# A two-layer mixer and a two-layer transformer block in float32 on one core: x and ctx fetched ahead of the weights, conditioning in two 32-column parts, value products in runs of two pairs

## Chip, cores and metric

One core of a Trainium2 chip. The metric is the device time of one execution in microseconds: the median of three runs before is 1947.4 (1946.05 to 1948.95). Outputs are float32.

## What is computed

x and ctx have 256 tokens of 1024 features. A first block has two layers of this form (a second block follows with two rounds of ffn1, mix, ffn2; the last norm ends the kernel):

```
mod   = silu(c) @ ada_w + ada_b          # shift, scale, gate for x
mod_c = silu(c_ctx) @ ada_w + ada_b      # the same for ctx
hx = rmsnorm(x, norm_w) * (1 + scale) + shift        # hc likewise from ctx
px, pc = split(hx @ w_in), split(hc @ w_in)
ya = global attention; yb = neighbourhood attention; yc = window attention
x = x + gate * ((concat(ya, yb, yc) * silu(px[9])) @ w_out)   # ctx too, in layer 0
```

In the second block, mix has two attentions: N (a compressed branch over 16 blocks, a selected and a window branch, gated) and M (causal), each with 8 heads, merged through w_branch and w_out. The compressed keys and values come from a small network with the weights cmpk_w1, cmpv_w1 and w2.

## The kernel before

Weights are stored as one packed array in the order of `weight_plan` (lines 108 to 141), in tiles of 128 x 1024 floats (512 KB). `_dma` (248) issues one tile on SP's queue, `_split` (272) makes a rounded part wh with ScalarE (286) and a remainder wl with VectorE (287), up to AHEAD = 2 tiles ahead of their use with three buffers each. `three` (424 to 428) multiplies float32 numbers as three products of rounded parts, accumulated in PSUM; every large product is made of these lines 426, 427 and 428. Python code emits the program, and a scheduler may put an instruction earlier than the text has it, once its tiles are free; each engine then runs its own instructions in order.

**The start** (`start`, 833). SP's queue fetches two weight tiles, x, four tiles, ctx, two tiles, the constants, then tiles up to 18. x and ctx are normalized in place (842 to 844). The shift and scale of layer 0 come in two groups of two column blocks (`ADA_HALF`, 56), eight tiles each. The first group (tiles 0 to 7, `START_PLAIN`) multiplies unsplit float32 weights by a stationary operand of 8 columns (747), into 8 rows of one PSUM bank. The second group is split and uses two products (750, 752), interleaved with the gate projection of chunks 0 to 3 (`gate`, 851; 96 matmuls of line 424's kind in four banks over both halves). `ada_close` (756) copies the bank to SBUF (762), selects and transposes it with the constant sel2 (765) and adds the bias. `half` (846) transposes x and ctx (800), applies scale and shift (809) and splits the result into hT (812, 813), half of the feature chunks at a time. The later groups (`ADA_FILL`, 57) run inside layer 0's gate projections; two of them hold the gate part of the modulation.

**Attention** (`attention`, 502). A unit holds one or two slots of scores; two units make a pair of heads. For each slot: scores (514, 515), softmax (`f_m`, `f_n`), transposes of the weights into PSUM (580), a copy to the tile pt (596, 598; three buffers). `f_v` (600) multiplies pt by V for one pair: line 609, plain float32, two 64-column parts of the array in turn, into 256 columns of the single bank "o". It is called when both units of the pair have been copied, or in a loop behind the last slot (639, 644). In N, the second pair member adds the compressed branch (`extra`, 1372), products with 64 rows and 128 columns. Layer 0 has 4 bundles of 8 units and 4 of 4; layer 1 4 of 4 and 4 of 2; each mix 2 of 4 and 4 of 2. Attention, preparation and projections are interleaved by lanes with estimated costs (`q`, 306; `step`, 317).

**The end of a layer** (1097 to 1143). The gate of each stream is spread over 128 partitions by TensorE: 24 matmuls with a broadcast stationary column (1116) and VectorE copies (1117). Since the buffers of x and ctx serve as storage for the gate projection in layer 0 (`sg`, 888 to 892), both are fetched again (1110). `add` (1119) then multiplies and adds.

**The mix** (1188). The compression weights w1 (two loads of 1 MB in runs of 512 bytes, 1205) and w2 (1218) are issued on ScalarE's queue when the mix opens. `compress` (1227) uses them. fw2, the last norm's weight, is issued at the stage i = 1 (1516).

Of the kernel before, what the change touches and what calls it, by code (L numbers as in the profile page):

```python
# [15 lines left out]
ALU = mybir.AluOpType  # L16
# [43 lines left out]

START_TILES = 18
START_PLAIN = range(8)
START_LOADS = (2, 6, 8, START_TILES)
# [44 lines left out]
def weight_plan():  # L108
# [3 lines left out]
    n = len(a[1]) // 2  # L112
    plan += a[0] + g[0][:1] + a[1][:n] + g[0][1:] + a[1][n:] + g[1]
# [44 lines left out]
def const_table():  # L158
# [39 lines left out]
    e = np.arange(32)[:, None]  # L198
# [30 lines left out]
class Body:  # L229
# [272 lines left out]
    def attention(self, units, evac):  # L502
# [97 lines left out]
        def f_v(x):  # L600
            pair = units[x:x + 2]
            O = self.ps("o")[:, :2 * P]
            extra = pair[1].get("extra")
            nk = len(pair[0]["v"])
            for k in range(nk):
                for i in (1, 0):
                    u = pair[i]
                    v, b, m, c = u["v"][k]
                    nc.tensor.matmul(O[HD * i:HD * i + HD, c:c + m * P], v, u["pt"][:, b:b + m, :].rearrange("p m t -> p (m t)"),  # L609
                                     start=k == 0, stop=k == nk - 1 and extra is None)  # L610
            if extra is not None:
                extra(O)
            evac(O, pair[1])
# [13 lines left out]
        for s in range(n):  # L627
# [11 lines left out]
            while nv < len(units) and ends[nv + 1] < s:  # L639
                f_v(nv)  # L640
                c += 430 * len(units[nv]["v"])
                nv += 2
            yield c
        while nv < len(units):
            f_v(nv)
            nv += 2
            yield 430.0
# [91 lines left out]
    def ada_tile(self, g):  # L739
# [5 lines left out]
        for i, kk in enumerate(ks):  # L745
            if plain:
                self.nc.tensor.matmul(g["bank"][:4 * nb, :], self.cst1[:, kk, w], h[:, i, :],  # L747
                                      start=g["n"] == 0 and i == 0, stop=g["n"] == g["last"] and i == len(ks) - 1)
                continue
# [6 lines left out]
    def ada_close(self, g):  # L756
# [5 lines left out]
        nc.scalar.copy(m[:4 * nb, :], g["bank"][:4 * nb, :])  # L762
        p = self.ps("r")
        for j in range(4):
            nc.tensor.matmul(p[:, 16 * j:16 * j + 2 * nb], m[:4 * nb, j * P:(j + 1) * P],
                             self.cst("sel2")[:4 * nb, :2 * nb], start=True, stop=True)
        pv = p[:, :64].rearrange("p (j b s) -> p s b j", b=8, s=2)
        b = 0
        while b < nb:
# [4 lines left out]
            for s in range(2):  # L774
# [5 lines left out]
                if a < z:  # L780
                    nc.vector.scalar_tensor_tensor(self.mod[l][:, s, a:z], self.mod[l][:, s, a:z], 1.0,
                                                   self.col("norm_w", 8 * l + a - 8, z - a), op0=ALU.add, op1=ALU.mult)
            b = e

# [35 lines left out]
    def block1(self, x):  # L820
        nc, tc = self.nc, self.tc
        cx = self.cx1
        with ExitStack() as es:
            hp = es.enter_context(tc.tile_pool(reuse_waits="tile", name="hT", bufs=1))
            hT = self.new_hT(hp, 0)
            with tc.tile_pool(reuse_waits="tile", name="w0", bufs=START_TILES) as self.w0:
                self.start(x, cx, hT)
# [5 lines left out]
    def start(self, x, cx, hT):  # L833

        nc, tc = self.nc, self.tc
        for n, (t, nm) in zip(START_LOADS, ((x, "x"), (cx, "ctx"), (self.consts[0], "consts"), (None, None))):
            while self.di < n:
                self._dma()
            if nm:
                d = self.dram[nm]  # L840
                nc.sync.dma_start(t, d if nm == "consts" else d.rearrange("o (t p) d -> p (o t) d", p=P))
        nc.vector.tensor_copy(self.ident_r, self.ident)
        self.norm_rows(x, x)
        self.norm_rows(cx, cx)

        def half(h):
            for c in (4 * h, 4 * h + 2):
                for s, v in enumerate((x, cx)):
                    self.mod_pair(0, s, c, self.turn_pair(v, c), hT)

        def gate(h, i, n):
            ks, _, wh, wl = self.w_next("w_in", 0, 3072 + 256 * i)
            for a, kk in enumerate(ks):
# [3 lines left out]
                for _ in range(n):  # L857
                    yield

        self.fill, self.fills = None, list(ADA_FILL)  # L860
        g = self.ada_open(ADA_HALF[0], "m")
        for i in range(8):
            self.ada_tile(g)
        self.ada_close(g)
        half(0)
        self.gate_acc = [self.acc() for _ in range(GATE_HALF)]
        g = self.ada_open(ADA_HALF[1], "m")
        for i in range(GATE_HALF // 2):
            for _ in gate(0, i, 1):
                self.ada_tile(g)  # L870
        self.ada_close(g)
        self.cond1.close()
        half(1)
        for i in range(GATE_HALF // 2):
            for _ in gate(1, i, 0):
                pass
# [4 lines left out]
    def layer1(self, l, x, cx, hT, hp):  # L881
# [3 lines left out]
        with ExitStack() as lay:  # L885
            lp = lay.enter_context(tc.tile_pool(reuse_waits="tile", name=f"lay{l}", bufs=1))
            if need:
                sg2 = lp.tile([P, 4, T], F32, name="sg2")
                xv, cv = (t.rearrange("p t (a d) -> p (t a) d", d=T) for t in (x, self.cx1))

                def sg(c, n):
                    return (xv, cv, sg2)[c // 4][:, c % 4:c % 4 + n, :]
# [17 lines left out]
            sink = lp.tile([P, 8], F32, name=f"sink{l}")  # L910
# [3 lines left out]
            nsink = lp.tile([P, 8], F32, name=f"nsink{l}")  # L914
# [185 lines left out]
            with tc.tile_pool(reuse_waits="tile", name=f"wo{l}", bufs=1) as wp:  # L1100
                gate = wp.tile([P, 2, D], F32, name=f"gt{l}")
                tmp = wp.tile([P, 4, 512], F32, name=f"tmp{l}")
                if need:
# [5 lines left out]
                    for t, nm in ((x, "x"), (cx, "ctx")):  # L1109
                        nc.sync.dma_start(t, self.dram[nm].rearrange("o (t p) d -> p (o t) d", p=P))  # L1110
# [519 lines left out]
```

## Time and profile before

| | |
|---|---|
| profiled execution | 1947.63 us, span 1945.8 |
| TensorE | 1904.4 us busy, 98% |
| weight loads of TensorE | 1561.0 us, 80% |
| VectorE, ScalarE | 1279.4 us (66%), 1103.3 us (57%) |
| GpSimd | 1.0 us |
| granted clock, mean | 0.992 |
| DMA | 294.62 MB, 151 GB/s |

Times in the trace are microseconds from the first instruction. A matmul's end is modelled, and consecutive ones overlap, so the time that one takes of the engine is read from start to start.

### The profile page before, as it was taken

The page shows a single profiled execution, that of the slowest core. Times are in us where ns is not written, and L with a number is a line of the kernel's source. Part 1 is how long each engine was busy: PE and PEld are TensorE (multiplying, and loading weights), DVE is VectorE, ACT ScalarE, POOL GpSimd, SP SyncE. Part 2 cuts the span into 40 slices and gives each one's busy share as a digit, 9 for nine tenths or more (in the row PEclk, how much of TensorE's full clock was granted, in tenths as well). Part 3 has the DMA queues.
Part 4 walks back from the last instruction along what each step waited for, and adds up shares of the span by engine and source line. Part 5 has one row for each costly group of instructions (what it writes and reads, how often), then busy time and mean ns, then how long its engine had stood idle before and what let it go on. Part 6 is the DMA issues. An engine that isn't in the chain of part 4 may idle for free.

```text
span 1945.8 us, 27694 instructions
## 1 busy us (share of the span) xinstructions
PE 1904.4 (98%) x10348; PEld 1561.0 (80%) x10348; DVE 1279.4 (66%) x2490; ACT 1103.3 (57%) x1979; POOL 1.0 (0%) x7
## 2 busy tenths in 40 slices
PE   8999999999999999999899999999999899999998
PEld 3777778777988877888788878888888788888886
DVE  5486856788596787555689575555555588675555
ACT  4367657775567675444467645445444458655443
POOL 0000000000000000000000000000000000000000
PEclk9999999999999999999999999999999999999999
DMA  7333324135422236554523565554555433456552
GB/s 304 106 123 130 118 90 150 55 131 186 136 93 95 85 109 216 184 184 141 166 93 125 164 215 198 183 191 173 193 186 173 144 106 101 152 180 234 186 181 74
DMA packets 85270, 294.62 MB, mean 151 GB/s; under 512 B 10000, under 2 KB 10384, under 8 KB 85136
## 3 DMA queue, kind: packets, MB, share of 16 engines
q1 hardware_dynamic: 80432, 283.39, 43.0%
q10 hardware_dynamic: 4704, 9.47, 1.5%
q8 instruction: 81, 1.33, 0.3%
q14 instruction: 53, 0.43, 0.1%
HBM read 291.77 MB, written 1.05 MB: 150 GB/s over the span
## 4 chain that ended last, share of the span: by engine, by line
PE 92%; DVE 4%; ACT 2%; issue 1%; ACTq 1%; DMA 1%; SPq 0%; DVEq 0%
PE acc L426 24%; PE acc L428 24%; PE acc L427 24%; PE pso L609 4%; PE pst L580 4%; PE pss L514 2%; PE pss L515 2%; PE psr L715 1%; DVE wl L287 1%; PE psx L1173 1%; ACT wh L286 1%; PE psr L721 1%; PE psm L747 1%; PE psm L1260 1%; PE acc L750 1%
## 5 line engine op out<-in xcount | busy, mean ns | idle before, releaser
L287 DVE TENSOR_TENSOR wl<-ws,wh 128x1024 fp32r<-128x1024 f32 (+2 forms) x538 | 638.1, 1188 | 478.8 <-ACT wh L286 476.0
L286 ACT CAST wh<-ws 128x1024 fp32r<-128x1024 f32 (+2 forms) x538 | 549.2, 1024 | 573.3 <-PE acc L428 503.3
L426 PE MATMUL acc<-wh,xt 128*128 128x512 f32 (+3 forms) x1120 | 419.6, 376 | 11.7 <-ACT wh L286 11.7
L427 PE MATMUL acc<-wl,xt 128*128 128x512 f32 (+3 forms) x1120 | 416.6, 372 | 0.0
L428 PE MATMUL acc<-wh,xt 128*128 128x512 f32 (+3 forms) x1120 | 416.4, 373 | 0.0
L426 PEld LDWEIGHTS acc<-wh,xt 128*128 128x128 f32 x1120 | 212.1, 190 | 44.9 <-ACT wh L286 12.9
L428 PEld LDWEIGHTS acc<-wh,xt 128*128 128x128 f32 x1120 | 211.8, 189 | 33.0 <-issue 0.7
L427 PEld LDWEIGHTS acc<-wl,xt 128*128 128x128 f32 x1120 | 212.7, 190 | 31.2 <-issue 0.3
L426 PE MATMUL acc<-wh,hT 128*128 128x384 f32 (+2 forms) x480 | 159.6, 333 | 0.1
L427 PE MATMUL acc<-wl,hT 128*128 128x384 f32 (+2 forms) x480 | 158.5, 330 | 0.0
L428 PE MATMUL acc<-wh,hT 128*128 128x384 f32 (+2 forms) x480 | 158.1, 329 | 0.0
L550 ACT ACTIVATE p<-pss,nm 128x512 f32<-128x512 f32 (+2 forms) x240 | 127.5, 539 | 20.3 <-DVE nm L546 5.1
L426 PE MATMUL acc<-wh,hffn 128*128 128x512 f32 x352 | 137.7, 391 | 0.0
L428 PE MATMUL acc<-wh,hffn 128*128 128x512 f32 x352 | 137.1, 389 | 0.0
L427 PE MATMUL acc<-wl,hffn 128*128 128x512 f32 x352 | 137.0, 389 | 0.0
L580 PE MATMUL pst<-consts,p 128*128 128x128 f32 x624 | 103.3, 278 | 0.0
L427 PEld LDWEIGHTS acc<-wl,hT 128*128 128x128 f32 x480 | 90.6, 189 | 7.2 <-issue 1.9
L426 PEld LDWEIGHTS acc<-wh,hT 128*128 128x128 f32 x480 | 90.5, 189 | 6.8 <-issue 0.8
L428 PEld LDWEIGHTS acc<-wh,hT 128*128 128x128 f32 x480 | 90.5, 189 | 5.8 <-issue 1.2
L580 PEld LDWEIGHTS pst<-consts,p 128*128 128x128 f32 x624 | 72.2, 140 | 28.5 <-ACT p L572 5.6
L572 ACT ACTIVATE p<-p,rinv 128x256 f32<-128x256 f32 (+2 forms) x152 | 81.5, 573 | 16.5 <-DVE rinv L566 12.2
L428 PEld LDWEIGHTS acc<-wh,hffn 128*128 128x128 f32 x352 | 66.1, 188 | 13.9
(318 smaller groups left out, 2868.5 us busy)
## 6 DMA issues: line engine op xcount, KB each, us to landing
ws<-in_wall SPq DMA_DIRECT2D x476, 512.0 KB, 3.4
ws<-in_wall SPq DMA_DIRECT2D x64, 384.0 KB, 3.1
bias<-in_bias ACTq DMA_DIRECT2D x8, 512.0 KB, 4.0
x<-in_x SPq DMA_DIRECT2D x2, 1024.0 KB, 6.5
cx<-in_ctx SPq DMA_DIRECT2D x2, 1024.0 KB, 10.3
ws<-in_wall SPq DMA_DIRECT2D x4, 420.0 KB, 3.0
out<-y SPq DMA_DIRECT2D x2, 512.0 KB, 2.6
ws<-in_wall SPq DMA_DIRECT2D x2, 280.0 KB, 2.8
```

What stands on the lines that cost most here:

```text
L286: self.nc.scalar.copy(h[:, :n], s[:, :n])
L287: self.nc.vector.tensor_tensor(lo[:, :n], s[:, :n], h[:, :n].bitcast(F32), op=ALU.subtract)
L426: mm(out, ah, bh, start=start, stop=False)
L427: mm(out, ah, bl, start=False, stop=False)
L428: mm(out, al, bh, start=False, stop=stop)
L514: nc.tensor.matmul(S[:, o:o + w], q, kh, start=True, stop=False)
L515: nc.tensor.matmul(S[:, o:o + w], q, kl, start=False, stop=True)
L550: nc.scalar.activation(p[:, o:o + w], S[:, o:o + w], AF.Exp, bias=nm[:, i:i + 1], accum_out=sm[:, i:i + 1])
L572: nc.scalar.activation(p[:, o:o + w], p[:, o:o + w], AF.Copy, scale=r[:, i:i + 1])
L580: nc.tensor.transpose(t[:, i * P:(i + 1) * P], sl["P"][:, o:o + P], self.ident)
L609: nc.tensor.matmul(O[HD * i:HD * i + HD, c:c + m * P], v, u["pt"][:, b:b + m, :].rearrange("p m t -> p (m t)"), start=k == 0, stop=k == nk ...
L715: nc.tensor.transpose(p[:, 2 * a + g, :], ks[:, t, a, g, :], self.ident_r)
```

## The change

- Start: x, the identity part of the constants and ctx are fetched ahead of all weight tiles; the rest of the constants follows tile 8. Normalized rows go to new tiles, so x stays as it was. Both groups of layer 0 are plain float32; the two matmuls of a tile go to the column parts 0 to 31 and 32 to 63, into 64 rows, and sel2 (now 64 rows) adds the parts up. The order of tiles is first group, first gate tile, second group, the other gate tiles.
- Attention: `f_v` takes two pairs (four units) into the two halves of the bank, the second pair first; it is called once four units are ready. pt has five buffers. The compressed branch becomes products of 128 rows (zeros in 64 of them) and 64 columns inside the same run; its tiles are padded to 128.
- The gate rows are written to DRAM from POOL's queue (`gate_rows`) and read back as a broadcast on ScalarE's queue, in place of lines 1112 to 1117. x is not fetched again; ctx is.
- w1 and w2 are issued in ffn1, after its second wg product (`cmp_load`), into tiles of the second block's pool; fw2 at i = 2.

```
-START_PLAIN = range(8)
+START_PLAIN = [*range(8), *range(9, 17)]
...
-    plan += a[0] + g[0][:1] + a[1][:n] + g[0][1:] + a[1][n:] + g[1]
+    plan += a[0] + g[0][:1] + a[1] + g[0][1:] + g[1]
...
-                u["pt"] = self.pp.tile([P, 8, P], F32, tag="pt", name=f"pt_{self.uid}", bufs=3)
+                u["pt"] = self.pp.tile([P, 8, P], F32, tag="pt", name=f"pt_{self.uid}", bufs=5)
...
+        def f_v(x, n):
+            pairs = [(units[x + 2 * j], units[x + 2 * j + 1], 2 * P * j) for j in range(n)]
+            O = self.ps("o")
+            todo = []
+            for pair in pairs[::-1]:
+                for k in range(len(pair[0]["v"])):
+                    for i in (1, 0):
+                        v, b, m, c = pair[i]["v"][k]
+                        todo.append((i, c + pair[2], m * P, v, pair[i]["pt"][:, b:b + m, :].rearrange("p m t -> p (m t)")))
+            for pair in pairs[::-1]:
+                todo += [(i, c + pair[2], P, v, p) for i, c, v, p in pair[1].get("extra", [])]
+            for y, (i, c, w, v, p) in enumerate(todo):
+                nc.tensor.matmul(O[HD * i:HD * i + HD, c:c + w], v, p, start=y < 2, stop=y >= len(todo) - 2)
+            for pair in pairs:
+                evac(O[:, pair[2]:pair[2] + 2 * P], pair[1])
...
-            while nv < len(units) and ends[nv + 1] < s:
-                f_v(nv)
-                c += 430 * len(units[nv]["v"])
-                nv += 2
+            if nv + 3 < len(units) and ends[nv + 3] < s:
+                f_v(nv, 2)
+                c += 860 * len(units[nv]["v"])
+                nv += 4
...
+                g["rows"] = 64
+                self.nc.tensor.matmul(g["bank"][32 * i:32 * i + 32, :], self.cst1[:, kk, 28 - 4 * b:60 - 4 * b], h[:, i, :],
+                                      start=g["n"] == 0, stop=g["n"] == g["last"])
...
+    def gate_rows(self, l, c0, n):
+        if l not in self.gates:
+            self.gates[l] = self.gp.tile([2, KD, P], F32, name=f"gates{l}")
+        c = c0 // P
+        for s in range(2 if l == 0 else 1):
+            self.nc.gpsimd.dma_start(self.gates[l][s, c:c + n // P, :].rearrange("j p -> p j"), self.mod[l][:, s, 16 + c:16 + c + n // P])
...
+        nc.sync.dma_start(x, self.dram["x"].rearrange("o (t p) d -> p (o t) d", p=P))
+        nc.sync.dma_start(self.consts[0][:, :P], self.dram["consts"][:, :P])
+        nc.sync.dma_start(cx, self.dram["ctx"].rearrange("o (t p) d -> p (o t) d", p=P))
+        while self.di < 8:
+            self._dma()
+        nc.sync.dma_start(self.consts[0][:, P:], self.dram["consts"][:, P:])
...
+        cond(0)
         half(0)
         self.gate_acc = [self.acc() for _ in range(GATE_HALF)]
...
+        gate(0, 0)
+        cond(1)
         self.cond1.close()
+        gate(0, 1)
         half(1)
...
-                sg2 = lp.tile([P, 4, T], F32, name="sg2")
-                xv, cv = (t.rearrange("p t (a d) -> p (t a) d", d=T) for t in (x, self.cx1))
+                sgs = [lp.tile([P, 4, T], F32, name="sg0"), cx.rearrange("p t (a d) -> p (t a) d", d=T),
+                       lp.tile([P, 4, T], F32, name="sg2")]
...
-                    for ct in range(2):
-                        p = self.ps("x")
-                        for j in range(4):
-                            g = self.mod[l][:, s, 16 + 4 * ct + j:17 + 4 * ct + j]
-                            nc.tensor.matmul(p[:, j * P:(j + 1) * P], g.to_broadcast([P, P]), self.ident, start=True, stop=True)
-                        nc.vector.tensor_copy(gate[:, s, ct * 512:ct * 512 + 512], p)
+                    g = self.gates[l][s:s + 1].rearrange("s j p -> s (j p)")
+                    nc.scalar.dma_start(gate[:, s, :], g.to_broadcast([P, D]))
...
+                if fi == 1 and name == "ffn1":
+                    self.cmp_load(l)
...
+                        scp = mp.tile([P, 2, 8, 16], F32, tag="scmp", name=f"scmp{l}{b}")
+                        nc.gpsimd.memset(scp, 0.0)
+                        sc = scp[:, :, :4, :]
...
+                            extra = [(i, j * P, Vb[:, b, 2 * j + i, :], pcT[:, t, :]) for j in range(2) for i in (1, 0)]
...
-            if i == 1:
+            if i == 2:
```

## Rows read from the trace of the kernel before

**Rows 1.** The page: shares of the chain that ended last; one DMA issue group.
```profile
PE 92%; DVE 4%; ACT 2%; issue 1%; ACTq 1%; DMA 1%; SPq 0%; DVEq 0%
...
bias<-in_bias ACTq DMA_DIRECT2D x8, 512.0 KB, 4.0
```

**Rows 2.** Timeline of TensorE, start: start us, us, engine line op out<-in xcount [idle before <-releaser].
```profile
6.43 16.32 PE L747 MATMUL psm<-ws,cst 128*8 128x512 f32 x32 [6.43 <-DMA ws<-in_wall]
...
49.95 1.05 PE L765 MATMUL psr<-consts,mod 8*128 8x4 f32 x8 [1.41 <-ACT mod L762]
...
54.86 2.07 PE L426 MATMUL acc<-hT,wh 128*128 128x512 f32 x4
...
67.85 0.39 PE L426 MATMUL acc<-wh,hT 128*128 128x512 f32 x1
```

**Rows 3.** Timeline of TensorE's weight loads, first conditioning group.
```profile
10.65 0.13 PEld L747 LDWEIGHTS psm<-ws,cst 128*8 128x8 f32 x1 [0.72 <-issue]
...
17.42 0.09 PEld L747 LDWEIGHTS psm<-ws,cst 128*8 128x8 f32 x1 [0.34 <-issue]
...
20.44 0.09 PEld L747 LDWEIGHTS psm<-ws,cst 128*8 128x8 f32 x1 [0.34 <-DMA ws<-in_wall]
```

**Rows 4.** Windows: stretch, length, busy us of each engine, PEclk, DMA share, GB/s.
```profile
10.00:20.00 10.00, 10.00 (x23) 1.85 (x21) 3.53 (x15) 4.64 (x15) 0.00 (x0) 1.00 1.03 410
...
945.00:950.00 5.00, 0.44 (x1) 0.35 (x2) 1.19 (x2) 1.88 (x4) 0.00 (x0) 0.66 1.04 285
```

**Rows 5.** Timeline of TensorE around one set of V matmuls in layer 1.
```profile
613.32 0.40 PE L427 MATMUL acc<-wl,hT 128*128 128x512 f32 x1
613.64 1.95 PE L609 MATMUL pso<-pt,VG 128*64 128x256 f32 x16
615.52 0.50 PE L428 MATMUL acc<-wh,hT 128*128 128x512 f32 x1
615.85 0.39 PE L426 MATMUL acc<-wh,hT 128*128 128x512 f32 x1
616.08 0.39 PE L427 MATMUL acc<-wl,hT 128*128 128x512 f32 x1
```

**Rows 6.** Timeline of TensorE: the first, a broken and the last V piece.
```profile
137.03 1.95 PE L609 MATMUL pso<-pt,VG 128*64 128x256 f32 x16
...
143.79 0.65 PE L609 MATMUL pso<-pt,VG 128*64 128x256 f32 x4
...
1673.82 0.87 PE L609 MATMUL pso<-pt,mVX 128*64 128x256 f32 x8
```

**Rows 7.** Timeline of TensorE: the compressed branch in the first mix.
```profile
1015.80 0.49 PE L1374 MATMUL pso<-pcT,Vb 64*128 64x128 f32 x2
...
1027.09 0.71 PE L1374 MATMUL pso<-pcT,Vb 64*128 64x128 f32 x4
```

**Rows 8.** Line 609: what TensorE's idle time ahead of it waited for (us, times).
```profile
  DVE pt L598: 6.3, 19
```

**Rows 9.** Timeline of all engines at the end of layer 0.
```profile
435.48 1.06 PE L1116 MATMUL psx<-consts,mod 128*128 128x128 f32 x8
...
442.04 0.68 DVE L1117 COPY gt<-psx 128x512 f32<-128x512 f32 x1
```

**Rows 10.** Timeline of ScalarE and its queue at the first mix.
```profile
940.17 0.85 ACTq L1205 DMA_DIRECT2D w<-in_cmpk_w  x1
...
944.59 3.41 ACTq L1218 DMA_DIRECT2D w<-in_cols  x1
948.12 1.39 ACT L286 CAST wh<-ws 128x560 fp32r<-128x560 f32 x2 [6.67 <-issue]
```

**Rows 11.** Waits of TensorE, 935 to 960 us: waited for, us in total, times, longest.
```profile
PE acc L426 <- ACT wh L286: 5.0, 1, 5.0
```

**Rows 12.** Timeline of ScalarE and its queue in the first ffn1.
```profile
765.13 0.35 ACTq L1518 DMA_DIRECT2D fw<-in_final_norm  x1
...
787.10 1.37 ACT L1161 ACTIVATE sffn<-acc,rr 128x512 f32<-128x512 f32 x2 [0.99 <-PE acc L428]
```

More of the change, by code (lines that the diff above doesn't have):

```diff
@@ L598, in f_e @@
                 nc.vector.tensor_copy(dst, src)
[L600 to L613, printed above, removed]
+        def f_v(x, n):
[13 more added lines that the diff above has]
+                evac(O[:, pair[2]:pair[2] + 2 * P], pair[1])
         ends, e = [], -1
@@ L825, in block1 @@
             hT = self.new_hT(hp, 0)
-            with tc.tile_pool(reuse_waits="tile", name="w0", bufs=START_TILES) as self.w0:
-                self.start(x, cx, hT)
+            with tc.tile_pool(reuse_waits="tile", name="w0", bufs=START_TILES) as self.w0, \
+                    tc.tile_pool(reuse_waits="tile", name="xn0", bufs=1) as xp:
+                self.start(x, cx, hT, xp)
             for l in range(DEPTH):
@@ L831, in block1, with start, gate @@
                 hT = self.layer1(l, x, cx, hT, hp)
-    def start(self, x, cx, hT):
+    def start(self, x, cx, hT, xp):
         nc, tc = self.nc, self.tc
[L836 to L841, printed above, removed]
+        nc.sync.dma_start(x, self.dram["x"].rearrange("o (t p) d -> p (o t) d", p=P))
[4 more added lines that the diff above has]
+        nc.sync.dma_start(self.consts[0][:, P:], self.dram["consts"][:, P:])
+        while self.di < START_TILES:
+            self._dma()
         nc.vector.tensor_copy(self.ident_r, self.ident)
-        self.norm_rows(x, x)
-        self.norm_rows(cx, cx)
+        xn, cn = (xp.tile([P, 2, D], F32, name=f"xn0_{j}") for j in range(2))
+        self.norm_rows(x, xn)
+        self.norm_rows(cx, cn)
         def half(h):
             for c in (4 * h, 4 * h + 2):
-                for s, v in enumerate((x, cx)):
+                for s, v in enumerate((xn, cn)):
                     self.mod_pair(0, s, c, self.turn_pair(v, c), hT)
-        def gate(h, i, n):
+        def gate(h, i):
             ks, _, wh, wl = self.w_next("w_in", 0, 3072 + 256 * i)
@@ L1143, in layer1, with cmp_load @@
                 return hT
+    def cmp_load(self, l):
+        nc = self.nc
+        w1 = [self.bp.tile([P, 16, P], F32, tag=f"big{j}", name=f"w1{l}_{j}") for j in range(2)]
+        for j, nm in enumerate(("cmpk_w1_2", "cmpv_w1_2")):
+            nc.scalar.dma_start(w1[j], self.dram[nm][l].rearrange("(m p) j -> p m j", p=P))
+        w2 = self.bp.tile([P, 2, HD], F32, tag="w2", name=f"w2{l}")
+        o2 = COLS["w2"][0] + P * l
+        nc.scalar.dma_start(w2, self.dram["cols"][:, o2:o2 + P].rearrange("p (a d) -> p a d", a=2))
+        self.cmp_w = w1, w2
     def ffn(self, l, name, x, xt, ss, hooks, after):
@@ L1390, in attn_lane @@
                                 vv = [v[:, m, j, :] for j in range(2) for m in range(t + 1)]
[L1391 removed]
+                                units.append(self.unit(sl, [(x, 2 * y, 2, 0) for y, x in enumerate(vv)], extra=extra if r else [], tok=t))
                         def ev(O, sl, b=b):
```

83 lines of the change are left out of this document (33 added, 50 removed).

## The prediction

> **What bounds the kernel now.** I read the page first. By its first lines TensorE is busy for 98% of the span, and the chain that ended last is 92% TensorE [rows 1], so time goes away only where TensorE matmuls are removed, or where its column stream is broken: by a wait, a change of tile shape or the low clock. From there I went through the stretches that the diff touches.
>
> The start [rows 2]: the first conditioning group is 32 instructions of 512 columns, from 6.43 to 22.8 us (16 matmuls in the source; a plain float32 matmul is two instructions). Layer 0's first projection begins at 67.85. At the lower clock (1.2 GHz) one instruction takes 0.85 us (0.13 + 0.72), at the higher one 0.43 (0.09 + 0.34), and the last weight tile is waited for until 20.44 [rows 3]: this group is already paced by the DMA at 410 GB/s [rows 4], 1.28 us per tile of 512 KB. Between 22.8 and 67.85 TensorE has 96 gate matmuls at 0.227 us (21.8), 32 conditioning matmuls at 0.23 (7.3), two sets of selections (1.0 each) and 32 transposes at 0.11 (3.5): 34.6 of 45.0 us. The other 10.4 are waits for ScalarE (such as 1.41 ahead of 49.95) and matmuls at 0.43 instead of 0.23 at the lower clock, as after 54.86 [rows 2].
>
> The V matmuls (line 609): 64 columns wide, two at a time in the two halves of the array. A plain float32 instruction costs 0.43 us for 512 columns, so 0.213 for 256; the 16 of rows 5 take 1.88 us, 0.117 each [rows 5]. Two halves run nearly at once. But each visit has a price: the instruction before it takes 0.32 instead of 0.227, the 16 take 1.88 instead of 8 x 0.213 = 1.71, the instruction behind it 0.33 instead of 0.227. **That is 0.37 us per piece.** By the code there are 24 + 12 + 8 + 8 = 52 visits; in the TensorE timeline they are 66 pieces from 137.03 to 1673.82, since some are broken up, as the one that shows x4 [rows 6].
>
> The start of each mix [rows 10, 11]: three loads for the compression weights hold ScalarE's queue from 940.17 to 948.0; the weight copies stand behind them, TensorE waits 5.0 us for one, and the granted clock is 0.66 in that stretch [rows 4], so it comes back at the lower of its two levels (1.2 GHz). With about 1.7 us for that (0.66 means some 3.4 of 5 us at half speed) a mix start loses 6.7 us; the second mix has the same three issues.
>
> **The change part by part.**
>
> *Start.* x, the identity and ctx now lie ahead of the weights on SP's queue, so the first tile lands later: 2 x 1.05 MB and 0.07 MB less the 1.05 MB that stood ahead of it with two tiles; from 6.43 and 20.44 I work out 11.6 us for the first tile and 20.7 for the eighth (the bytes ahead of the eighth are nearly the same). With two 32-column parts, as the V rows show, the two matmuls of a tile take 0.85 us at the higher clock, 1.7 at the lower; arrival at 1.28 lets it catch up, and the group ends at 21.6 instead of 22.8. After that the work is 1.0 + 1.8 + 10.9 + 6.8 (the second group, 16 x 0.853 / 2) + 1.0 + 1.8 + 10.9 = 34.2 us, against 34.6. The gain is in the waits: the second group needs no split, so ScalarE (1.05) and VectorE (1.22 per tile) have 8 of 12 tiles fewer in the way of hT, and the closing of the second group lies beside the second gate tile. I keep 6.6 of the 10.4 us, so the projection begins at 62.4: **-5.5**. Bounds: all stalls stay, -1; nearly none, -9.
>
> *V runs.* 52 visits become 12 + 8 + 6 + 6 = 32. If they break as often as now (66/52), 41 pieces, 25 x 0.37 = 9.3 less; if never, 34 x 0.37 = 12.6. A run that begins with its youngest pair is ready as a whole, which speaks for few breaks; but in the attention stretches VectorE shares the bound, so I take **-8.5**. Bounds: -12.6, and 0 if the later start eats it. Five pt buffers carry the four units that now wait. *Compressed part* (line 1374): a 64-row shape costs two more switches. Four instructions take about 0.64 us of the 0.71 shown, and where they stand alone in twos 0.57 each [rows 7]; as four column-half matmuls inside the run 8 x 0.107 / 2 = 0.43. One of four per mix stands in twos: 0.7 + 3 x 0.2 = 1.3 per mix, **-2.5**. Line 1304 keeps the full shape: 2 x 0.37 = **-0.7**. The memset on POOL has an idle engine and 400 ns of other work ahead of its reader; its cost if that goes is some 0.3 us, four times.
>
> *Gate rows.* 24 matmuls are 48 instructions of 0.112 (1.06 us for the eight of rows 9, one of six such sets): 5.4 us of TensorE, and 6 VectorE copies of 0.68 [rows 9]. The first group lies at 435.48, where TensorE would wait for the last attention anyway; of the four sets in layer 0 I count two (1.9), and all of layer 1's 1.8. Against that ScalarE's queue issues three broadcasts of 512 KB (each 0.35, as fw [rows 12]); a load of that size on that queue lands after 4.0 us [rows 1], beside the ctx reload perhaps after 6, and the add that reads it in layer 0 stands behind 24 matmuls of 0.227, 5.4 us, so VectorE may wait 1. **-3.5**; bounds -5.4 and +2. The small writes on POOL's queue come with the fill groups, in the middle of layer 0; their price is shown nowhere, and nothing behind them on that queue is waited for. *x kept*: one 1 MB reload less beside the ctx one: **-0.3**, bounds 0 and -1.
>
> *Compression weights.* The same three issues move to the first ffn, and ScalarE is held 7.9 us there too. TensorE then has up to three split tiles of 12 x 0.227 = 2.72: 8.2 us, of which the last copy (1.05) has used some. Behind the loads come two Silu (1.37) [rows 12], a copy (1.05), then its subtraction: 1.05 + 7.9 + 1.37 + 1.05 - 8.2 = 3.2 us late, about 4.2 with the low half. So 6.7 - 4.2 = 2.5 per mix, **-5** in all. The loads may also be issued earlier than the text of the program has them: the row of fw stands at 765 although its line comes after the first ffn [rows 12]. Bounds: hidden, -13.4; a busier place for ScalarE, +3.
>
> **Sum**: -5.5 - 8.5 - 2.5 - 0.7 - 3.5 - 0.3 - 5 = -26. Against the profiled execution, 1947.63 (span 1945.8 and 1.8 around it; 0.2 above the median of the three runs, so the same), that is **1921.5 us**.
>
> A rule against the first term: the Trainium skill, page "TensorE: Matmul & The Clock Gate", section "Measured speedup vs the span model", gives 2.38 for three column parts, not 3. The V rows show nearly 2 for two inside a run and are the nearer measure. By the page's ratio two parts would give an estimated 1.6, the second group would take 8.6 us instead of 6.8, and the time would be near 1923.5.
>
> **The rivals.**
>
> *Column parts do not overlap* in the conditioning groups, since nothing here runs 32-column parts of different halves. For it: the only rows are 64 wide. Against it: rows 5. Price: the first group ends at 27.8 instead of 21.6, the second takes 13.7 instead of 6.8: +13, **1934.5**.
>
> *The loads cost as much in the ffn* as at the mix (ScalarE held when TensorE has nothing split), and the runs break up: 5 + 5, **1931.5**. For it: rows 10 show the issues themselves to be long, and rows 6 the breaking.
>
> *The loads are hidden whole* and no run breaks: -8.4 - 4.1, **1909**. For it: VectorE and ScalarE are half idle in the ffn; against it the queue's 7.9 us.
>
> *It does not do what it says*: the scheduler puts other matmuls between the two pairs of a run, so pieces stay at 66: **1930**.
>
> *Slower: a run waits for its youngest unit.* Each of the 32 runs begins with the pair whose pt copy is the last in ScalarE's or VectorE's order. Today TensorE's idle ahead of line 609 for that copy is 6.3 us in 19 cases, 0.33 each [rows 8]. If no projection matmul stands between the last transposes and the run, the wait is four transposes at 0.11, a copy of 512 columns at 0.68 (the shape of the second line of [rows 9]) and the hand-offs, some 1.4 us; 32 x 1.4 = 45 in place of the gain gives **1975**. It decides from 0.8 us per run (26/32); against it, projections fill most of these stretches.
>
> **How the numbers follow.** Forecast 0.57, loads hidden 0.13, loads not cheaper 0.13, pieces as before 0.06, parts not overlapping 0.05, slower by waits 0.06. The forecast's own range is 1914 to 1930; the others at 0.13 and 0.06 stretch it to **1907 to 1939**, leaving out the waits and the far ends. About 0.2% (3.9 us) is what a measurement of this kernel can tell from no change. Faster 0.91; same 0.03 (two of the bad cases together, or weak waits); slower 0.06.
>
> **What would show it.** The projection's first matmul at about 62; some 40 pieces of 64-wide V matmuls or fewer, at 0.37 around each; no broadcasting matmuls at 435 and 737; no 5 us wait ahead of the mixes, but one of 3 to 4 us in each first ffn. Wrong would be: a first group past 25 us, idle TensorE of a microsecond ahead of the runs, or VectorE waiting for gate rows.

## The result and the profile after

The changed kernel took **1920.26 us** (median of four runs, 1919.23 to 1921.19), the kernel before 1946.8 beside it (1946.05 to 1948.95): a ratio of 0.9862, 95% interval 0.9845 to 0.9879, so 1.2% to 1.6% faster. Forecast: 1921.5, range 1907 to 1939. The profiled execution took 1919.23 (span 1917.4) against 1947.63.

The page of the changed kernel, its first lines and the chain that ended last ([rows 1] showed 92% of TensorE, 4% of VectorE):

```profile
span 1917.4 us, 27602 instructions
...
PE 1876.4 (98%) x10332; PEld 1549.6 (81%) x10332; DVE 1263.4 (66%) x2476; ACT 1094.2 (57%) x1971; POOL 4.9 (0%) x14
...
PE 90%; DVE 6%; ACT 2%; DMA 1%; issue 1%; SPq 0%; ACTq 0%; DVEq 0%
```

TensorE still sets the end. Both kernels run the same 7248 product matmuls, so the start of the n-th of them can be compared stage by stage. The table gives how much earlier the changed kernel starts it (worked out from both profiled executions), and what the stage adds:

| stage (start in the changed kernel, us) | earlier by, us | of which in this stage |
|---|---|---|
| layer 0's first projection (65.05) | 2.8 | 2.8 |
| past the end of layer 0 (473) | 10.3 | 7.5 |
| late in layer 1 (674) | 13.1 | 2.8 |
| past the end of layer 1 (758) | 12.0 | -1.1 |
| inside the first mix (979) | 18.2 | 6.2 |
| end of the first mix (1343) | 19.9 | 1.7 |
| inside the second mix (1564) | 26.8 | 6.9 |
| end | 28.6 | 1.8 |

*Start*, TensorE's timeline of the changed kernel, the counterpart of [rows 2]:

```profile
12.10 7.37 PE L748 MATMUL psm<-ws,cst 128*32 128x512 f32 x24 [12.10 <-DMA ws<-in_wall]
...
20.97 1.05 PE L748 MATMUL psm<-ws,cst 128*32 128x512 f32 x4 [0.22 <-DMA ws<-in_wall]
...
26.22 1.91 PE L748 MATMUL psm<-ws,cst 128*32 128x512 f32 x2
...
37.07 6.20 PE L748 MATMUL psm<-ws,cst 128*32 128x512 f32 x26
...
52.29 0.66 PE L812 MATMUL psx<-consts,xn 128*128 128x128 f32 x4 [1.28 <-ACT ht L821]
...
54.03 1.20 PE L423 MATMUL acc<-hT,wh 128*128 128x512 f32 x4 [0.17 <-DVE hT L824]
...
65.05 0.39 PE L423 MATMUL acc<-wh,hT 128*128 128x512 f32 x1
```

The first group ends at 22.0, near the forecast (21.6), and still waits for its last tiles by DMA. Six instructions of the second group were drawn ahead into gaps between the transposes, where they run in twos and some at the lower clock (26.22: 1.91 us for two): from start to start these six take 3.9 us, the other 26 take 6.1. The gate tile of the second half begins at 54.03, where the kernel before began it at 54.86: nearly all that was gained by then is gone. ScalarE's timeline tells why: hT's second half (line 821) begins only at 51.22, though its coefficients are copied at 43.34.

```profile
43.34 0.58 ACT L764 COPY mod<-psm 64x512 f32<-64x512 f32 x1 [7.54 <-PE psm L748]
...
50.27 1.05 ACT L283 CAST wh<-ws 128x1024 fp32r<-128x1024 f32 x1 [4.45 <-PE acc L424]
51.22 1.92 ACT L821 ACTIVATE ht<-psx,mod 128x256 f32<-128x256 f32 x4
```

The granted clock ([rows 4] had 1.00 and 0.66; columns as there; the last row is the start of the first mix, which stood at 945 to 950 before):

```profile
10.00:20.00 10.00, 7.64 (x26) 1.76 (x28) 6.97 (x30) 3.08 (x10) 0.00 (x0) 1.00 1.03 410
20.00:30.00 10.00, 8.51 (x36) 3.44 (x32) 4.89 (x13) 5.10 (x10) 0.00 (x0) 0.83 1.03 409
...
935.00:940.00 5.00, 5.00 (x35) 5.00 (x35) 3.33 (x6) 3.91 (x7) 0.00 (x0) 1.00 0.55 174
```

*V runs*, TensorE's timeline in layer 1 ([rows 5]), and two pieces of the first mix, where the compressed branch now is ([rows 6, 7]):

```profile
619.24 0.39 PE L424 MATMUL acc<-wl,hT 128*128 128x512 f32 x1
619.56 1.95 PE L609 MATMUL pso<-pt,VB 128*64 128x256 f32 x16
621.44 0.50 PE L425 MATMUL acc<-wh,hT 128*128 128x512 f32 x1
...
1006.57 2.81 PE L609 MATMUL pso<-pt,mVX 128*64 128x256 f32 x24
1009.21 1.04 PE L609 MATMUL pso<-pcT,Vb 128*64 128x128 f32 x16
```

A piece of layer 1 costs what it did: 0.32 in front, 1.88 for sixteen, the next 0.11 longer. In the mixes a piece of eight is cheaper, before and after: the one of [rows 6] at 1673.82 are followed in the kernel before by

```profile
1674.62 0.50 PE L427 MATMUL acc<-wl,xt 128*128 128x512 f32 x1
```

so its eight take 0.80, less than the 4 x 0.213 = 0.85 of the working, and with 0.1 lost on either side the piece costs 0.15. (Eight in layer 0 take 1.02, from 275.28 to 276.30 in the kernel before.) There are 37 pieces, where the kernel before had 66 and four more of the compressed branch (70 stretches with line 1374's taken in). Waits for the copies did not grow; the line by operation ([rows 8]: 6.3, 19) now reads:

```profile
  DVE pt L595: 6.1, 19
```

*Gate rows*, VectorE at the end of layer 1, with what TensorE then waits for ([rows 9] showed the broadcasts they replace):

```profile
732.89 1.29 DVE L1132 TENSOR_TENSOR tmp<-acc,gt 128x512 f32<-128x512 f32 x2 [2.51 <-DMA gt<-gates]
...
739.72 0.41 PE L464 MATMUL psx<-consts,x 128*128 128x128 f32 x2 [1.56 <-DVE x L1133]
```

*Compression weights*, ScalarE and its queue ([rows 10, 12] showed 3.41 us for the last issue and Silu at 787.10):

```profile
722.80 0.84 ACTq L1160 DMA_DIRECT2D w<-in_cmpk_w  x1
...
728.13 0.71 ACTq L1160 DMA_DIRECT2D w<-in_cmpv_w  x1
...
739.72 0.34 ACTq L1163 DMA_DIRECT2D w<-in_cols  x1
...
775.09 1.37 ACT L1183 ACTIVATE sffn<-acc,rr 128x512 f32<-128x512 f32 x2 [0.98 <-PE acc L425]
```

They are not in the ffn, where their line stands just ahead of the Silu at 775.09 (the 787.10 of before), but 35 to 52 us earlier, apart from each other, and short; those of the second mix stand at 965, 1108 and 1113, as short. All that TensorE waits for at the mix, 915 to 945 us ([rows 11]: 5.0 for a split):

```profile
PE acc L424 <- DVE wl L284: 0.3, 1, 0.3
```

### The profile page after: what moved, and what is told of

It is laid out like the page before. It is cut to its first block, busy times and chain, and to the rows that moved or that the text cites. A ratio compares the mean times of both kernels' runs of the same rounds, so it can differ in the third digit from the quotient of the medians.

```text
span 1917.4 us, 27602 instructions
## 1 busy us (share of the span) xinstructions
PE 1876.4 (98%) x10332; PEld 1549.6 (81%) x10332; DVE 1263.4 (66%) x2476; ACT 1094.2 (57%) x1971; POOL 4.9 (0%) x14
## 4 chain that ended last, share of the span: by engine, by line
PE 90%; DVE 6%; ACT 2%; DMA 1%; issue 1%; SPq 0%; ACTq 0%; DVEq 0%
PE acc L423 24%; PE acc L425 24%; PE acc L424 23%; PE pso L609 4%; PE pst L577 4%; PE pss L511 2%; PE pss L512 2%; DVE wl L284 2%; PE psr L714 1%; PE psx L1195 1%; PE psr L720 1%; PE psm L1277 1%; DMA ws<-in_wall 1%; PE acc L751 1%; PE acc L753 1%
## 5 line engine op out<-in xcount | busy, mean ns | idle before, releaser
L284 DVE TENSOR_TENSOR wl<-ws,wh 128x1024 fp32r<-128x1024 f32 (+3 forms) x530 | 628.0, 1187 | 455.9 <-ACT wh L283 454.7
L283 ACT CAST wh<-ws 128x1024 fp32r<-128x1024 f32 (+3 forms) x530 | 541.4, 1024 | 531.3 <-PE acc L425 476.9
L569 ACT ACTIVATE p<-p,rinv 128x256 f32<-128x256 f32 (+2 forms) x152 | 81.3, 577 | 11.6 <-DVE rinv L563 8.5
```

The lines of the kernel that those rows point to most:

```text
L283: self.nc.scalar.copy(h[:, :n], s[:, :n])
L284: self.nc.vector.tensor_tensor(lo[:, :n], s[:, :n], h[:, :n].bitcast(F32), op=ALU.subtract)
L569: nc.scalar.activation(p[:, o:o + w], p[:, o:o + w], AF.Copy, scale=r[:, i:i + 1])
```

## The experiments

Twelve kernels, each the changed kernel with one edit (best1: two). "Earlier" and "later" are starts of the same product matmul against the changed kernel's profiled execution, if nothing else is said. One execution is not exact to a microsecond at the start: in the changed kernel's the first weight tile came at 12.10 and layer 0's projection at 65.05, while seven kernels below whose edit lies behind the start (both on the gate rows, the three on the compression weights, both on the V runs) have the tile at 11.5 to 11.7 and the projection at 63.41 to 64.56, median 64.25. These seven are the second measure of the start. The runs come from three chips, on which the kernel before took 1946.02 (half_first to w1_at_mix), 1946.84 (w1_mix_pool to one_pair) and 1944.81 (no_overlap to best1), so medians of different chips compare to about 2 us.

**half_first**: the second half of hT ahead of the second gate tile.

```diff
-        gate(0, 1)
-        half(1)
+        half(1)
+        gate(0, 1)
```

> The changed kernel with half(1) emitted ahead of gate(0, 1). Theory: the start fell 2.7 us short of the forecast because the second half of hT was written only from 51.22 us on, behind a gate tile that does not need it; with the two swapped the first gate tile of the second half begins at about 51 instead of 54.0, layer 0's first projection at about 62.5 instead of 65.05, and the time is 1917.5 (2 to 3 us below the changed kernel's 1920.3). Rival: the transposes wait for ScalarE ahead of the gate tile in place of behind it, the projection begins at 65 again and the time stays at 1920.

Measured: 1917.09 us (1915.86 to 1917.57), ratio 0.9847 [0.9829, 0.9864]. Its projection:

```profile
61.96 0.39 PE L423 MATMUL acc<-wh,hT 128*128 128x512 f32 x1
```

3.1 us earlier, and 2.3 earlier than the median of the seven. The theory holds: the place of half(1) is worth some 2.3 us at the start, and by the medians 1.7 against w1_at_mix (below) on the same chip, 3.2 against the changed kernel's own runs.

**gates_pe_l1** and **gates_pe**: layer 1's rows by TensorE again, or (without the condition) both layers'.

```diff
+                    if not need:
+                        for ct in range(2):
+                            p = self.ps("x")
...
+                            nc.tensor.matmul(p[:, j * P:(j + 1) * P], g.to_broadcast([P, P]), self.ident, start=True, stop=True)
+                            nc.vector.tensor_copy(gate[:, s, ct * 512:ct * 512 + 512], p)
+                        continue
```

> The changed kernel with layer 1's gate rows written by TensorE and VectorE again, layer 0's by DMA. The prediction's term for it: 1.8 us of TensorE come back, so the time is 1922. Theory from the trace of the changed kernel: the DMA version waits 2.5 us on VectorE for the rows that land 6 us after their issue, and TensorE 3.4 us for what follows, so writing them on TensorE costs 1.8 and gives back 2.5 to 3.4: 1919, and VectorE's wait for the rows ahead of the first product at the end of layer 1 is gone. Rival: the three waits of TensorE (3.4 us together) are those of the adds themselves and stay; then 1922.

> The changed kernel with the gate rows of both layers written by TensorE and VectorE again. The prediction's term: 3.5 us come back, 1924. Theory: layer 0's part was right (1.9 us of TensorE come back), layer 1's was a loss (1 us is gained), so 1921. Rival: in layer 0 the broadcasts wait for the last attention anyway, so that only layer 1 shows: 1919.

Measured: 1919.1 us (1918.13 to 1919.8) and 1921.92 (1921.22 to 1922.84); w1_at_mix below, which keeps the changed kernel's work and nearly its order, took 1918.78 (1918.28 to 1918.99) on the same chip. So layer 1's part is worth 0.3 us, which is within the spread of the runs, both together 3.1. In gates_pe's trace layer 0's end alone takes 2.3 more. My theory's 1919 came, but by luck: against w1_at_mix nothing was gained. VectorE's wait of 2.51 went, but the wait of TensorE ahead of line 464 shrank only from three of 0.69, 1.56 and 1.12 to one of 1.9, and the matmuls took back the rest:

```profile
PE psx L464 <- DVE x L1141: 1.9, 1, 1.9
```

(waits of TensorE, gates_pe_l1). The prediction's term of 3.5 was nearly right in sum.

**w1_at_mix**: the call moved back to the mix, its buffers left where the change put them.

```diff
-                if fi == 1 and name == "ffn1":
-                    self.cmp_load(l)
...
+            self.cmp_load(l)
             w1, w2 = self.cmp_w
```

> The changed kernel with the compression weights loaded at the start of each mix again, all three issues on ScalarE's queue. The prediction's term: 5 us come back, 1925. Theory from the trace of the changed kernel: the three issues again stand back to back and hold ScalarE some 7.9 us, each mix start loses 6 to 7 us (a wait of TensorE for a split of about 5 us at each, granted clock near 0.66), 13 in all, of which up to 4 come back at the end of layer 1, where the loads now lie beside the gate rows: 1929 to 1933. Rival: the loads at the end of layer 1 cost nothing there: 1933; or the issues are spread here too by the order that the scheduler now finds: 1921.

Measured: 1918.78 us, ratio 0.9856 [0.9835, 0.9877]. The last rival holds: in its trace the three issues stand at 721.83, 727.18 and 739.28, as in the changed kernel. The text's place of the call does nothing; the next run shows that the buffers' pool decides (that the issues go out as soon as their buffers are free is my reading of it). That spoiled it as an undo, so:

**w1_mix_pool**: the loads' buffers, and graw, which shares them, in the mix's own pools again, as in the kernel before. **w1_mix_pool_sp**: the same, with the three issues on SP's queue (nc.sync for nc.scalar).

```diff
-            w1, w2 = self.cmp_w
+            w1 = [op.tile([P, 16, P], F32, tag=f"big{j}", name=f"w1{l}_{j}") for j in range(2)]
+            for j, nm in enumerate(("cmpk_w1_2", "cmpv_w1_2")):
+                nc.scalar.dma_start(w1[j], self.dram[nm][l].rearrange("(m p) j -> p m j", p=P))
...
+            w2 = mp.tile([P, 2, HD], F32, name=f"w2{l}")
+            o2 = COLS["w2"][0] + P * l
+            nc.scalar.dma_start(w2, self.dram["cols"][:, o2:o2 + P].rearrange("p (a d) -> p a d", a=2))
...
```

> The changed kernel with the compression weights in buffers of the mix's own again (as the kernel before has them), so that their three loads cannot be issued before the mix opens. The run before this one showed that the place of the call in the text does not place the issues: they go out as soon as their buffers are free. Theory: the three issues stand back to back at the mix, hold ScalarE some 7.9 us, and each mix start loses 6 to 7 us (a wait of TensorE for a split of about 5 us, granted clock near 0.66); 13 in all, less up to 4 that the end of layer 1 gets back: 1929 to 1933. The prediction's term: 5 us, 1925. Rival: the mix starts are short now for another reason (the final weights' load that was moved from one feed-forward to the other, other buffers), 1920.

> As w1_mix_pool, with the three loads issued on SP's queue instead of ScalarE's. If it is ScalarE's engine being held by the issues that costs the time, the mix starts keep what they gained and the time is 1920 (at most 1923, if SP's own weight loads come late by the issues). If it is the transfers or the buffers coming free late, it is as in w1_mix_pool, 1929 to 1933. A third way: SP is held as ScalarE was, its prefetch of weights falls behind, and TensorE waits for DMA in place of the split: 1925 or more, with waits for ws ahead of the mix.

Measured: 1929.52 us (1927.78 to 1930.26), ratio 0.9915 [0.9899, 0.9932], and 1918.44 (1917.74 to 1919.1), 0.986 [0.9846, 0.9875], on one chip. ScalarE and its queue at the first mix of w1_mix_pool:

```profile
925.80 0.85 ACTq L1225 DMA_DIRECT2D w<-in_cmpk_w  x1
...
927.10 3.58 ACTq L1225 DMA_DIRECT2D w<-in_cmpv_w  x1
930.72 3.19 ACTq L1238 DMA_DIRECT2D w<-in_cols  x1
934.04 1.39 ACT L283 CAST wh<-ws 128x560 fp32r<-128x560 f32 x2 [6.96 <-issue]
```

TensorE's waits there (925 to 940 us):

```profile
PE acc L423 <- ACT wh L283: 5.3, 1, 5.3
```

The granted clock behind it, in the windows of the same kernel:

```profile
930.00:935.00 5.00, 0.20 (x2) 0.00 (x0) 0.27 (x1) 0.96 (x2) 0.00 (x0) 0.80 0.96 273
935.00:940.00 5.00, 4.52 (x17) 4.06 (x18) 4.51 (x16) 3.30 (x10) 0.00 (x0) 0.52 0.69 225
```

The two mix starts lose 6.6 and 6.0 us in the matched matmuls, the end of layer 1 gets 1.2 back. With SP as issuer the issues at the same place are nearly as long in sum,

```profile
924.48 0.84 SPq L1225 DMA_DIRECT2D w<-in_cmpk_w  x1
925.77 2.65 SPq L1225 DMA_DIRECT2D w<-in_cmpv_w  x1
928.47 3.44 SPq L1238 DMA_DIRECT2D w<-in_cols  x1
```

but the mix starts lose only 0.7 and 1.3. The bytes, their place and their buffers are the same in both; what differs is whose queue the issues hold. That ScalarE is held ahead of a split is the cause, shown, with 11.1 us between the two. The Trainium skill, page "Perfetto Trace Analysis", section "DMA Optimizations", says that balancing DMAs across the issuing engines may help where an engine looks busy with descriptor generation. This pair bears on it in part only: the three issues went from the engine that computes to the queue that already issues the weights, so it shows the gain of freeing ScalarE, not of balance.

**pairs_forward** (older pair first in a run; the first edit) and **one_pair** (one pair in a run; the second).

```diff
-            for pair in pairs[::-1]:
+            for pair in pairs:
                 for k in range(len(pair[0]["v"])):
...
-            if nv + 3 < len(units) and ends[nv + 3] < s:
-                f_v(nv, 2)
+            while nv < len(units) and ends[nv + 1] < s:
+                f_v(nv, 1)
...
```

> The changed kernel with the two pairs of a run in the other order (older pair first). By the order of its instructions the V matmuls then stand in 76 pieces instead of 37. Theory: each piece costs 0.37 us of TensorE's stream, so 39 x 0.37 = 14.3 us come on top: 1934.5. Rival: a piece costs only where it breaks a stream that is otherwise full, and the pieces of a broken run stand between the score and transpose matmuls of the attention, where TensorE waits for other engines anyway: less than 5 us, 1925.

> The changed kernel with one pair of heads in a run, as before the change, the rest as changed. By the order of its instructions the V matmuls stand in 71 pieces instead of 37 (the kernel before: 66, and four of the compressed branch). Theory at 0.37 us per piece: 34 x 0.37 = 12.6 us, 1932.9. The prediction's terms for the runs and the compressed branch together: 11, of which this undoes 8.5 to 11: 1929 to 1931. Rival: shorter units in flight let the attention end earlier and give some of it back: 1925.

Measured: 1926.03 us (1925.61 to 1926.62), ratio 0.99 [0.9885, 0.9914], and 1925.48 (1924.54 to 1926.83), 0.9897 [0.9882, 0.9912]. The traces have the 76 and 71 pieces, some between the attention's own transposes, as here (one_pair, TensorE):

```profile
139.73 0.65 PE L609 MATMUL pso<-pt,VG 128*64 128x256 f32 x4
140.31 0.55 PE L577 MATMUL pst<-consts,p 128*128 128x128 f32 x3
140.79 1.51 PE L609 MATMUL pso<-pt,VG 128*64 128x256 f32 x12
142.24 0.66 PE L577 MATMUL pst<-consts,p 128*128 128x128 f32 x4
```

At 0.37 each that should cost 14.3 and 12.6; it cost 5.8 and 5.2 by the medians, 7.0 and 7.6 by the spans. Both full prices are refuted for the time as a whole; the rivals' 1925 is nearer, though the first one's bound of 5 us is passed. The matched matmuls show where the rest went, and most of it is not hidden among the attention's own matmuls: late in layer 1 (674 us) pairs_forward is 10.2 later with 33 more pieces, one_pair 9.0 with 24 more, or 0.33 and 0.42 per piece once their earlier starts (0.75 and 1.0) are added. Past the end of layer 1 they are only 6.9 and 5.6 later. Some 3.4 us are taken up there: VectorE does not wait for the gate rows in either of the two, and TensorE's waits of 3.4 ahead of line 464 are down to 2.0 and 1.1. In the mixes one_pair loses 2.0 more with its 8 pieces more.

**no_overlap**: both matmuls of a conditioning tile in one column part.

```diff
-                self.nc.tensor.matmul(g["bank"][32 * i:32 * i + 32, :], self.cst1[:, kk, 28 - 4 * b:60 - 4 * b], h[:, i, :],
-                                      start=g["n"] == 0, stop=g["n"] == g["last"])
+                self.nc.tensor.matmul(g["bank"][:32, :], self.cst1[:, kk, 28 - 4 * b:60 - 4 * b], h[:, i, :],
+                                      start=g["n"] == 0 and i == 0, stop=g["n"] == g["last"] and i == 1)
...
```

> The changed kernel with both matmuls of a conditioning tile in the same 32 columns (rows 0 to 31 of the bank, accumulating), so that two of them can't run at once. The prediction's rival without overlap gives its price: the first group ends 6.2 us later and the second takes 6.8 us more, 13 in all. From the trace of the changed kernel: 26 instructions of the second group took 6.20 us, in one column part 26 x 0.427 = 11.1, so 4.9 more; the first group, 32 instructions begun at the lower clock, ends at about 27 to 28 instead of 22.0: together 11, 1931. Rival: the first group waits for its tiles by DMA in either form and the later start is filled up by the splits that are then ready: 1926 or less.

Measured: 1927.73 us (1926.14 to 1930.11), ratio 0.9914 [0.9899, 0.9929].

```profile
11.50 15.41 PE L748 MATMUL psm<-ws,cst 128*32 128x512 f32 x32 [11.50 <-DVE rt L389]
...
38.41 12.20 PE L748 MATMUL psm<-ws,cst 128*32 128x512 f32 x28
...
72.10 0.39 PE L423 MATMUL acc<-wh,hT 128*128 128x512 f32 x1
```

28 instructions in 12.20 us (0.436 each) against 26 in 6.20 (0.238): two parts give 1.8, ends included. The projection comes 7.05 us later, 7.9 later than the median of the seven, not 11. The first group ends 4.9 later and the second costs 5 more, but the first gate product comes only 2.4 later (32.59, in the changed kernel 30.21): 2.5 us are taken up between the first group and that product, where the changed kernel waits for ScalarE and VectorE and runs two of the instructions drawn ahead at the lower clock (1.91 us, here 1.05). The hole that half_first closes is still there, with a wait of 0.95 us ahead of 59.33.

**tiles_first** (the first edit): the loads of the start in the order of before, the identity kept behind x. **cond1_split** (the second): the second group split in high and low as before.

```diff
+        while self.di < 2:
+            self._dma()
         nc.sync.dma_start(x, self.dram["x"].rearrange("o (t p) d -> p (o t) d", p=P))
         nc.sync.dma_start(self.consts[0][:, :P], self.dram["consts"][:, :P])
+        while self.di < 6:
+            self._dma()
         nc.sync.dma_start(cx, self.dram["ctx"].rearrange("o (t p) d -> p (o t) d", p=P))
...
-START_PLAIN = [*range(8), *range(9, 17)]
+START_PLAIN = range(8)
```

> The changed kernel with the loads of the start in the order of before: two weight tiles, x and the identity, four tiles, ctx, two tiles. Theory: the bytes ahead of the eighth tile are the same, so the first group ends at 22 again although it begins at about 6.5 instead of 12; only ctx is late by up to 5 us, its normalised copy too (18.4 now), which the transposes wait for at about 24.6: 1920 to 1922. Rival one: loading x and ctx first is what lets the group run without breaks at the higher clock, and the group that starts early runs at the lower one throughout: 1923 or more. Rival two: nothing at all changes, 1920.

> The changed kernel with the second conditioning group split in high and low parts as before (32 matmuls of 0.23 us, 7.3 us, and 8 more copies of 1.05 us on ScalarE and subtractions of 1.22 us on VectorE), its place in the order as changed. The prediction's reason for the gain of the start: the splits stand in the way of hT, so the waits come back: the projection begins 2.8 us later or more, 1923 to 1925. Rival: ScalarE is idle for 7.5 us and VectorE for 8 us ahead of the second group's end in the changed kernel's trace, so the splits fit and only 0.5 us of TensorE's own time comes on top: 1920.5.

Measured: 1919.24 us (1918.28 to 1922.43), 0.9872 [0.9858, 0.9887], and 1921.24 (1921.07 to 1921.57), 0.988 [0.9865, 0.9895]. tiles_first begins its first group at 6.24 and its projection at 65.97, 0.9 later than the changed kernel's and 1.7 later than the median of the seven; the medians show no change beyond the chips' 2 us. It waits for tiles in the middle of the group, 1.66 us ahead of 11.49 and then again:

```profile
19.17 3.22 PE L748 MATMUL psm<-ws,cst 128*32 128x512 f32 x8 [1.93 <-DMA ws<-in_wall]
```

The granted clock behind that, in the same kernel from 20 to 30 us:

```profile
20.00:30.00 10.00, 9.21 (x29) 4.53 (x28) 7.38 (x26) 4.09 (x9) 0.00 (x0) 0.50 1.03 410
```

cond1_split's projection is at 65.59, 0.5 later than the changed kernel's and 1.3 later than the median of the seven, its time 1.0 above the changed kernel's median. The rival is nearer: the splits mostly fit.

**best1**: half_first, and layer 1's gate rows fetched when the layer opens.

```diff
+                gate1 = lp.tile([P, 1, D], F32, name="gt1")
+                nc.scalar.dma_start(gate1[:, 0, :], self.gates[1][0:1].rearrange("s j p -> s (j p)").to_broadcast([P, D]))
...
```

> half_first, and layer 1's gate rows fetched from DRAM when the layer opens, into a buffer of the layer's own, instead of 6 us ahead of their use beside the compression weights. Theory: VectorE's wait of 2.5 us for them goes, of TensorE's waits of 4.1 us for the adds about 1.9 stay (as with the rows written by TensorE): 1915 (2 below half_first's 1917.1). Rival: the end of layer 1 is held by something else, VectorE's adds or the other transfers, and the time stays at 1917.

Measured: **1914.07 us** (1912.88 to 1916.36), ratio 0.9841 [0.9824, 0.9857]: 1.4% to 1.8% faster than the kernel before; its median is 6.2 below the changed kernel's, but by the ratios (0.9841 and 0.9862) the two are only 4 us apart. VectorE's wait for the rows is gone:

```profile
727.71 1.28 DVE L1134 TENSOR_TENSOR tmp<-acc,gt 128x512 f32<-128x512 f32 x2
```

TensorE's waits ahead of line 464 are down to one of 1.9. In the matched matmuls best1 gains 1.3 us on half_first at the end of layer 1 and loses 0.5 in layer 0, so most of the gain is half_first's. The medians come from different chips and the ratios (0.9841 and 0.9847) hardly differ, so how much of the 3 us between 1914.07 and half_first's 1917.09 is the fetch stays open. What it removes is not steady: five kernels that have the changed kernel's code there (half_first, w1_at_mix, no_overlap, tiles_first, cond1_split) show VectorE's wait for the rows at 3.0 to 4.0 us, where the changed kernel has 2.51, and spend 0.5 to 2.9 us more on the end of layer 1.

## Why the prediction was right, point by point

*Start, -5.5: it was -2.8* in the profiled execution, 3.6 by the median of the seven kernels with the same start. The group's end was nearly right (21.6, measured 22.0). Behind it the sum had 34.2 us of work and 6.6 of waits that stay, together 40.8; from 22.0 to 65.05 are 43.1. The step that failed: "the closing of the second group lies beside the second gate tile". It does, but hT's second half was issued behind that tile, and about 2.3 us of the 2.7 missing are that order (half_first began at 61.96, the forecast was 62.4). The second group's 6.8 was too low as well: it takes 10.0 of TensorE, part of them in gaps. The reason was wrong too: not the splits out of the way (about 1 us, cond1_split) but the overlap of the parts (7 to 8, no_overlap) carries the gain; without it the start would be 4.3 later than before, at 72.10 against 67.85. That rival's price of 13 was still too high, by 3 to 6: no_overlap is 7.5 above by the medians, 10 by the ratios, 7 by the profiles. By the Trainium skill ("TensorE: Matmul & The Clock Gate", "Measured speedup vs the span model") I had estimated 1.6 for two parts. What was measured is 1.8, ends included, and the V rows give the same by the same count: 16 x 0.213 in 1.88.

*V runs and compressed branch, -8.5 - 2.5 - 0.7.* 37 pieces came where I counted 41. By late in layer 1 the changed kernel is 13.1 us earlier, 8.0 without the start (2.8) and layer 0's gate rows (2.3): that is 0.35 for each of 23 pieces fewer, so price and term were right up to there. What reached the end was less, 5 to 8 us by the undoing of one part (one_pair), because the end of layer 1 takes 3.4 back. Of the mixes' share, 4.7 by my terms (four visits of 0.37, 2.5 and 0.7), 3.5 came. The mis-sized step is "0.37 us per piece" for all pieces: it was read between products of layer 1, and in the mixes a piece of eight costs 0.15, which makes the four visits 0.6 and the share 3.8. The wait for the youngest unit (the slower rival) is not there: 6.1 us in 19 cases, as before. No run undoes the compressed branch's form, the five pt buffers, x kept or the later fw2 by itself; their terms stand only in the sums of stages.

*Gate rows, -3.5:* measured 3.1, nearly all in layer 0. I had 1.9 there and 1.8 in layer 1, which with the wait of 1 us make 2.7 and not the 3.5 that I wrote. The wait that I put into layer 0 is not there, and in layer 1, where I had none, it was 2.5 us and ate that part.

*Compression weights, -5.* The step that failed: "The same three issues move to the first ffn, and ScalarE is held 7.9 us there too". The sentence further on ("may also be issued earlier") was the right one. They go out at 722 to 740, apart, at 0.84, 0.71 and 0.34 us, and both mix starts gain the 6.7 that I had read from [rows 10, 11] (6.2 and 6.9). Undoing it costs 9.3 us by the medians, 10.5 by the spans. The bound of -13.4 held it.

*Sum.* -26 was forecast, 26.5 came by the medians and 28.4 by the profiled executions, through errors of both signs: the start 2.7 too good, the loads 4 to 7 too bad, and 1.1 us lost at the end of layer 1 (beside the loads and the late gate rows), which was in no term. That the time came within 1.3 us of the forecast is in part luck. The rival "hidden whole" was right on the loads.

## What to carry to other kernels

A DMA's issue occupies the engine that issues it (ScalarE stood idle for 6.96 us in w1_mix_pool), so ask what stands behind it on that engine, and look at where the trace puts the issue, not at the line in the text. A price per break of TensorE's stream holds for the stream that it was read in (0.37 in layer 1, 0.15 for a piece of eight in the mixes), and a later wait can take up what the breaks cost: undo the edit once, and compare stage by stage. When work is reordered at a start, follow each producer to its place in the issuing order: one call emitted behind a tile that did not need it hid nearly half of the gain.

## What the runs showed of the hardware that was not expected

The issue of a load got longer the closer it stood behind the loads of 1 MB. The small load (in_cols) took 0.34 us when issued 11.6 us after them, 1.42 at 3.0 us (gates_pe_l1; 1.87 at 3.05 in gates_pe) and 3.19 to 3.73 right behind them, on ScalarE's and SP's queue alike; the second large one took 0.71 apart and 2.65 to 3.58 right behind the first. The distance is not all of it: the gate rows' broadcast, 4.0 us behind the first large load each time, took 0.34 to issue in the changed kernel, 0.74 in tiles_first and 1.58 in cond1_split. What sets it is not shown. Here gates_pe_l1's, beside the row above:

```profile
725.55 0.71 ACTq L1168 DMA_DIRECT2D w<-in_cmpv_w  x1
...
728.58 1.42 ACTq L1171 DMA_DIRECT2D w<-in_cols  x1
```

An earlier start of TensorE's first work was not an earlier end: in tiles_first the group began 6 us sooner, broke off for tiles (1.66 and 1.93 us), ended at 22.4 where the changed kernel's ended at 22.0, and the granted clock behind that was 0.50, its lower level (1.2 GHz).
